# Another order of the expert pairs in a mixture-of-experts stage: pairs of 96 and of 128 rows take turns

## The chip, the cores and the metric

One core of a Trainium2 chip runs the whole program as one launch. The metric is device microseconds of that launch, the median of several runs; less is better. The profile is one more execution, recorded by the hardware.

## What is computed

The reference is two blocks of a network on 256 tokens of width 1024, in float32. The first block (attention, a recurrent mixer, plain feed-forward layers) and the mixer of the second block come first and are not touched. What matters is the last stage, a mixture of 32 experts of which each token uses 4:

```python
def moe_ffn(h, router_w, router_b, w_gu, b_gu, w_down, b_down):
    logits = hf @ router_w + router_b
    top_logit, top_idx = lax.top_k(logits, TOP_K)          # 4 of 32
    gates = jax.nn.softmax(top_logit, axis=-1)
    ...
    def expert_block(args):
        xb, e = args
        y = clamped_swiglu(xb @ w_gu[e] + b_gu[e])         # 1024 x 2048
        return y @ w_down[e] + b_down[e]                   # 1024 x 1024
    ...
    out = jax.ops.segment_sum(y_rows * row_gate, row_tok)
```

The result is added to the residual and the sum is normalised. All 32 experts are used, so 32 x 12 MB of weights are read.

## The kernel before

The expert stage is the method `moe`, some 1000 us at the end of the program. A routing step ranks the experts 2 to 31 by the number of their tokens; experts 0 and 1 are fixed as the first two, so that their weights can be loaded before the routing is known. A **pair** is two ranks that are worked on together: the list `pairs` (L2086) puts rank 0 with rank 1, 64 rows each, and then rank 1 + b with rank 32 - b for b from 1 to 15. The first of the two has 96 rows for b below 8 and 64 rows from 8 on; the second always has 32. So there are seven pairs of 128 rows (ranks 2 to 8 in front), eight of 96 rows (ranks 9 to 16 in front), and the first with 64 + 64. Rows beyond an expert's place are left to a later branch (`moe_beyond`), which is not entered with these inputs.

The loop at L2280 walks through `pairs` in the order of the list. For each rank it reads the expert's number from a small table (`moe_expert`, L2322, on SyncE) and asks for its weights: `wload` (L146) issues eight loads of 1024 KB for the up projection and four for the down projection, each into one of 16 buffers of 1 MB that go round (tag `big`). SyncE (SP) issues these loads in order; a load waits until the matmuls of the load 16 places before have read their buffer, and for earlier loads on its lane. Nothing else moves in quantity, so the loads of weights run ahead of TensorE by at most 16 buffers, which is two thirds of a pair.

For each expert `up` (L2129) multiplies the gathered rows with the gate and up weights, adding the biases by small matmuls on `bgu` (L2144), and then forms the clamped product on DVE, ACT and POOL (L2161 to L2165). `down` (L2178) turns the product with the help of the identity (`turned`, L2173, evicted as `moeaT`), multiplies it with the down weights and scales it. The activations are the stationary operand and the weights stream: an expert of 64 rows streams 512 columns per matmul on half of the array, one of 32 rows 256 columns on a quarter. An expert of 96 rows is a part of 64 and one of 32, and reads every weight tile with both; so the time of TensorE for a tile grows with the rows, and the bytes do not.

While a pair is worked on, its first expert also carries the selection for the next pair (`pair`, `gather`, L2197, matmuls at L2207 into `xg`), and its second expert the addition of the previous pair's result (`scatter`, L2119). The closing activation of a pair is that of `put` at L175 on ACT. A scheduler that knows the dependences lays out each engine's instructions, so the gather's matmuls stand between others. In the pair after the first, `moe_bias` (L2345, matmuls at L2358) adds the biases of the down projection.

Of the kernel before, what the change touches and what calls it, by code (L numbers as in the profile page):

```python
# [50 lines left out]
class Kern:  # L51
# [2025 lines left out]
    def moe(self):  # L2077
# [5 lines left out]
        dn_of = lambda e: self.wload(wdn[e], 0, 8, 0, D)  # L2083


        pairs = [((0, 64), (1, 64))] + [((1 + b, 96 if b < 8 else 64), (32 - b, 32)) for b in range(1, 16)]  # L2086
        rows = dict(chain.from_iterable(pairs))
        most = lambda r: 256 if r < 2 else min(256, 1024 // (r - 1))
        first = [gu_of(0), dn_of(0), gu_of(1)]
# [465 lines left out]
```

## Time and profile before

| | us |
|---|---|
| median of 3 runs | 3098.86 |
| fastest and slowest of them | 3097.3 and 3103.04 |
| the profiled execution, its own time | 3102.66 |
| span of its records | 3100.9 |
| the first pair closes at | 2147.37 |
| the last pair closes at | 3079.49 |

A window is a stretch of the span. Its row gives its length, the busy time of each engine with the number of its instructions, the granted clock of TensorE as a share of full speed (0.5 is 1.2 GHz, 1.00 is 2.4 GHz; a number between is a mean over both), the busy share of the DMA engines and the bytes that they moved per second. A busy TensorE is not one at its peak, since its matmuls overlap. The clock of the whole span was 0.916. The windows by pair below are those of places 1 to 10, of place 15 and of the end behind it, place 0 being the pair of experts 0 and 1.

### The profile page before, as it was taken

The page shows a single profiled execution, that of the slowest core. Times are in us where ns is not written, and L with a number is a line of the kernel's source. Part 1 is how long each engine was busy: PE and PEld are TensorE (multiplying, and loading weights), DVE is VectorE, ACT ScalarE, POOL GpSimd, SP SyncE. Part 2 cuts the span into 40 slices and gives each one's busy share as a digit, 9 for nine tenths or more (in the row PEclk, how much of TensorE's full clock was granted, in tenths as well). Part 3 has the DMA queues.
Part 4 walks back from the last instruction along what each step waited for, and adds up shares of the span by engine and source line. Part 5 has one row for each costly group of instructions (what it writes and reads, how often), then busy time and mean ns, then how long its engine had stood idle before and what let it go on. Part 6 is the DMA issues. An engine that isn't in the chain of part 4 may idle for free. (4 is left out here: it accounts for less than half of the span.)

```text
span 3100.9 us, 47594 instructions
## 1 busy us (share of the span) xinstructions
PE 2765.1 (89%) x19070; PEld 1795.3 (58%) x19070; DVE 1490.4 (48%) x3210; ACT 882.5 (28%) x1827; POOL 517.4 (17%) x774
## 2 busy tenths in 40 slices
PE   7998989999979788987899988989999999998775
PEld 4873468888847555654798966763444433443332
DVE  4426465555567655764655878651222222222121
ACT  4223334223235343433454634530100000000001
POOL 0002310111100543543100322111100000000000
PEclk9998999999988897887899998989999999879887
DMA  6226741233221233432456323369999999999997
GB/s 227 96 92 211 273 144 55 95 95 95 86 86 42 75 108 98 108 95 81 144 190 204 118 62 113 125 248 360 381 411 382 373 377 372 416 417 416 416 417 290
DMA packets 254007, 650.74 MB, mean 210 GB/s; under 512 B 68816, under 2 KB 129616, under 8 KB 215376
## 3 DMA queue, kind: packets, MB, share of 16 engines
q1 hardware_dynamic: 239552, 632.96, 55.4%
q10 hardware_dynamic: 12432, 10.45, 1.1%
q0 software_dynamic: 1792, 4.20, 0.5%
q8 instruction: 152, 2.49, 0.3%
q14 instruction: 79, 0.65, 0.1%
HBM read 639.16 MB, written 8.39 MB: 209 GB/s over the span
## 5 line engine op out<-in xcount | busy, mean ns | idle before, releaser
L2126 PE MATMUL mm<-w,xg 128*32 128x256 f32 (+1 forms) x3904 | 434.2, 457 | 38.3 <-DMA w<-in_moe_w_gu_dram 38.3
L164 DVE TENSOR_TENSOR lo<-w,hi 128x512 fp32r<-128x512 f32 (+1 forms) x330 | 295.1, 927 | 107.7 <-ACT hi L163 93.4
L2126 PEld LDWEIGHTS mm<-w,xg 128*32 128x32 f32 (+1 forms) x3904 | 155.7, 120 | 306.0 <-issue 190.2
L163 ACT ACTIVATE hi<-w 128x512 fp32r<-128x512 f32 (+1 forms) x356 | 256.3, 770 | 236.5 <-PE tp L250 101.2
L2126 PE MATMUL mm<-w,moeaT 128*32 128x256 f32 (+1 forms) x1952 | 258.7, 500 | 8.7 <-DVE moeaT L95 3.8
L2162 ACT ACTIVATE moes<-moeg 128x256 f32<-128x256 f32 (+1 forms) x39 | 19.9, 510 | 653.6 <-DVE moeg L2161 653.6
L2161 DVE TENSOR_SCALAR moeg<-mm 128x256 f32<-128x256 f32 (+1 forms) x39 | 21.1, 541 | 349.7 <-PE mm L2126 349.3
L250 PE MATMUL mm<-mlo,hi 128*128 128x512 f32 (+1 forms) x512 | 173.4, 339 | 0.7 <-DVE mlo L173 0.7
L249 PE MATMUL mm<-mhi,hi 128*128 128x512 f32 (+1 forms) x512 | 173.1, 340 | 0.0
L251 PE MATMUL mm<-mhi,lo 128*128 128x512 f32 (+1 forms) x512 | 172.2, 337 | 0.0
L2126 PEld LDWEIGHTS mm<-w,moeaT 128*32 128x32 f32 (+1 forms) x1952 | 79.8, 128 | 140.8 <-issue 108.8
L251 PE MATMUL tp<-hi,aTl 128*128 128x512 f32 x384 | 151.7, 395 | 0.0
L250 PE MATMUL tp<-lo,aTh 128*128 128x512 f32 x384 | 151.3, 394 | 0.0
L249 PE MATMUL tp<-hi,aTh 128*128 128x512 f32 x384 | 151.1, 393 | 0.0
L2164 POOL TENSOR_TENSOR moeg<-moeg,moes 128x256 f32<-128x256 f32 (+1 forms) x39 | 37.4, 959 | 580.6 <-ACT moes L2162 566.0
L2195 DVE TENSOR_TENSOR moey<-mm,moegate 32x256 f32<-32x256 f32 (+1 forms) x122 | 60.5, 496 | 138.8 <-PE mm L2126 127.3
L164 POOL TENSOR_TENSOR lo<-w,hi 128x512 fp32r<-128x512 f32 (+1 forms) x26 | 51.8, 1994 | 348.0 <-ACT hi L163 293.9
L250 PEld LDWEIGHTS mm<-mlo,hi 128*128 128x128 f32 x512 | 96.4, 188 | 12.8 <-DVE mlo L173 1.1
L249 PEld LDWEIGHTS mm<-mhi,hi 128*128 128x128 f32 x512 | 96.0, 188 | 12.3 <-issue 0.5
L251 PEld LDWEIGHTS mm<-mhi,lo 128*128 128x128 f32 x512 | 96.3, 188 | 11.4
L2139 POOL TENSOR_SCALAR moesel<-moetk,moeown 128x320 fp32r<-128x320 f32 (+1 forms) x39 | 40.8, 1046 | 317.3 <-PE mm L2144 278.0
L249 PE MATMUL cv<-hT2h,hi 128*128 128x256 f32 x288 | 84.3, 293 | 8.8 <-DVE cvy L1754 8.8
(866 smaller groups left out, 5897.8 us busy)
## 6 DMA issues: line engine op xcount, KB each, us to landing
w<-in_moe_w_gu_dram SPq DMA_DIRECT2D x256, 1024.0 KB, 15.0
w<-in_moe_w_down_dram SPq DMA_DIRECT2D x128, 1024.0 KB, 16.6
w<-in_mlp_w_dram SPq DMA_DIRECT2D x64, 1024.0 KB, 5.4
w<-in_ada_w_dram SPq DMA_DIRECT2D x48, 1024.0 KB, 5.0
w<-in_w_in_dram SPq DMA_DIRECT2D x26, 1024.0 KB, 5.2
adaw<-in_ada_w_dram SPq DMA_DIRECT2D x48, 512.0 KB, 4.1
w<-in_ab_w_in_dram SPq DMA_DIRECT2D x14, 1024.0 KB, 5.1
w<-in_rw_w_rkv_dram SPq DMA_DIRECT2D x8, 1024.0 KB, 5.1
```

Source lines behind the costliest of these rows:

```text
L163: nc.scalar.activation(h, raw, AF.Copy)
L164: (eng or nc.vector).tensor_sub(l, raw, hi)
L249: nc.tensor.matmul(out, l[0], r[0], start=start, stop=False)
L250: nc.tensor.matmul(out, l[0], r[1], start=False, stop=False)
L251: nc.tensor.matmul(out, l[1], r[0], start=False, stop=stop)
L2126: return 8 * n, lambda p, c, l, r, s, st: nc.tensor.matmul(p[c * n:(c + 1) * n, :8 * n], l, r, start=s, stop=st, tile_position=(0, c * n))
L2139: nc.gpsimd.tensor_scalar(sel.bitcast(FR), takes[n], own[:, r:r + 1], None, op0=OP.mult)
L2161: nc.vector.tensor_scalar(g, pg[:, :w], 7.0, None, op0=OP.min)
L2162: nc.scalar.activation(s, g, AF.Sigmoid, scale=1.702)
L2164: nc.gpsimd.tensor_mul(g, g, s)
L2195: nc.vector.tensor_mul(y[:, cs], py[c * n:(c + 1) * n, :w], gate[c * n:(c + 1) * n, cs])
```

## The change

The list of pairs is written in another order. No pair is changed, and neither are the rows of a rank or the number of any instruction. After the first pair come the pairs with b = 8, 1, 9, 2, 10, 3, 11, 4, 12, 5, 13, 6, 14, 7, 15: of 96 rows, of 128, of 96, and so on, with one of 96 rows at the end. It was b = 15 at the end before, too.

```diff
-        pairs = [((0, 64), (1, 64))] + [((1 + b, 96 if b < 8 else 64), (32 - b, 32)) for b in range(1, 16)]
+
+        pairs = [((0, 64), (1, 64))] + [((1 + b, 96 if b < 8 else 64), (32 - b, 32))
+                                        for b in (8, 1, 9, 2, 10, 3, 11, 4, 12, 5, 13, 6, 14, 7, 15)]
```

Lines below it move by two. On SP the rows of the program stay as they were. On TensorE whole pairs change places. Just behind the first pair, TensorE before works on an expert of 96 rows; `w,xg` are products with the up weights (64x512 for a part of 64 rows, 32x256 for one of 32), `moebd,moeGT` the biases:

```order
L2126 MATMUL mm<-w,xg 64x512 x7
L2126 MATMUL mm<-w,xg 32x256 x13
L2358 MATMUL tp<-moebd,moeGT 128x512 x4
L2126 MATMUL mm<-w,xg 32x256 x3
L2126 MATMUL mm<-w,xg 64x512 x8
L2126 MATMUL mm<-w,xg 32x256 x16
```

The same place of the changed program, with the gather for the next pair (`moeoh,xnm`) behind it:

```order
L2128 MATMUL mm<-w,xg 64x512 x15
L2360 MATMUL tp<-moebd,moeGT 128x512 x4
L2128 MATMUL mm<-w,xg 64x512 x17
L2209 MATMUL tp<-moeoh,xnmh 128x128 x2
L2209 MATMUL tp<-moeoh,xnml 128x128 x2
```

The expert with 96 rows, eight tiles read by 32 + 64 matmuls in all, has made room for one of 64 rows with 32 matmuls (the trace shows two records for each of them); the biases' products stay in the first products of this pair.

The second place is on TensorE where the pair after a pair of 128 rows begins. Before it is another one of 128 rows (`moeaT` are the last down products of the pair that ends, 32 rows):

```order
L2126 MATMUL mm<-w,moeaT_18716 32x256 x8
L2207 MATMUL tp<-moeoh,xnml 128x128
L2207 MATMUL tp<-moeoh,xnmh 128x128 x2
L2207 MATMUL tp<-moeoh,xnml 128x128 x2
L2207 MATMUL tp<-moeoh,xnmh 128x128 x2
L2207 MATMUL tp<-moeoh,xnml 128x128
L2144 MATMUL mm<-bguh,moesel 128x256
L2144 MATMUL mm<-bgul,moesel 128x256
L2144 MATMUL mm<-bguh,moesel 128x256
L2144 MATMUL mm<-bgul,moesel 128x256
L2207 MATMUL tp<-moeoh,xnml 128x128
L2126 MATMUL mm<-w,xg 64x512 x4
```

In the changed program a pair of 96 rows begins there, its first expert in one piece, with the turning of its product and the scatter behind it:

```order
L2128 MATMUL mm<-w,moeaT_18590 32x256 x8
L2209 MATMUL tp<-moeoh,xnmh 128x128
L2209 MATMUL tp<-moeoh,xnml 128x128 x2
L2209 MATMUL tp<-moeoh,xnmh 128x128 x2
L2209 MATMUL tp<-moeoh,xnml 128x128 x2
L2128 MATMUL mm<-w,xg 64x512 x32
L2175 MATMUL tp<-ident,moeu_18721 128x128 x4
L2121 MATMUL tp<-moeyh,moegt 128x512
```

The second half of the biases for a part of 32 rows is gone there, and the eight up tiles of the pair follow in one run of matmuls.

## Rows read from the trace of the kernel before

**Rows 1.** The page, the span in 40 equal slices: rate of the transfers.
```profile
GB/s 227 96 92 211 273 144 55 95 95 95 86 86 42 75 108 98 108 95 81 144 190 204 118 62 113 125 248 360 381 411 382 373 377 372 416 417 416 416 417 290
```

**Rows 2.** Windows by pair: length; PE, PEld, DVE, ACT, POOL busy; clock; DMA share; GB/s.
```profile
2147.40:2214.30 66.90, 63.88 (x562) 29.27 (x562) 19.29 (x40) 4.58 (x9) 11.53 (x11) 0.95 0.84 330
2214.30:2279.30 65.00, 61.42 (x583) 30.72 (x581) 16.62 (x37) 6.12 (x13) 7.08 (x7) 0.97 1.02 416
2279.30:2343.10 63.80, 58.29 (x552) 25.83 (x552) 16.87 (x36) 4.82 (x9) 5.80 (x6) 1.00 1.01 408
2343.10:2411.30 68.20, 62.81 (x552) 27.58 (x552) 16.28 (x35) 5.31 (x10) 5.80 (x6) 0.92 0.94 379
2411.30:2479.70 68.40, 62.83 (x552) 27.49 (x552) 16.87 (x36) 4.84 (x10) 5.80 (x6) 0.93 0.92 367
2479.70:2548.60 68.90, 62.84 (x553) 27.68 (x553) 16.15 (x36) 5.26 (x11) 5.79 (x6) 0.93 0.93 372
2548.60:2617.50 68.90, 64.09 (x558) 27.34 (x560) 17.49 (x38) 5.46 (x11) 5.63 (x6) 0.93 0.92 366
2617.50:2665.80 48.30, 43.35 (x352) 20.82 (x350) 13.25 (x28) 4.54 (x9) 3.99 (x4) 0.96 1.02 418
2665.80:2724.20 58.40, 52.90 (x348) 26.18 (x346) 13.33 (x28) 4.49 (x8) 3.99 (x4) 0.77 1.02 416
2724.20:2786.00 61.80, 54.05 (x354) 25.62 (x352) 13.25 (x28) 4.55 (x9) 3.99 (x4) 0.78 1.02 417
...
3019.00:3079.50 60.50, 44.69 (x308) 15.92 (x304) 10.69 (x18) 2.80 (x5) 1.98 (x2) 0.86 0.92 374
3079.50:3100.90 21.40, 3.78 (x8) 2.48 (x8) 7.06 (x12) 6.40 (x9) 0.00 (x0) 0.50 0.21 78
```

**Rows 3.** Timeline of ACT: the closing activation of place 0 and of place 15.
```profile
2147.37 1.15 ACT L175 ACTIVATE moeyh<-moey,moetg 128x1024 fp32r<-128x1024 f32 x1 [10.03 <-DVE moey L2195]
...
3079.49 1.15 ACT L175 ACTIVATE moeyh<-moey,moetg 96x1024 fp32r<-96x1024 f32 x1 [10.92 <-DVE moey L2195]
```

**Rows 4.** The page, DMA issues: count, KB of each, us to landing.
```profile
w<-in_moe_w_gu_dram SPq DMA_DIRECT2D x256, 1024.0 KB, 15.0
w<-in_moe_w_down_dram SPq DMA_DIRECT2D x128, 1024.0 KB, 16.6
```

**Rows 5.** Waits of SP's queue (total, times, longest), first 2300 to 2620, then 2700 to 3060.
```profile
SPq L155 <- PE mm L2126: 240.8, 111, 9.9
...
SPq L155 <- DMA w<-in_moe_w_gu_dram: 106.4, 66, 2.4
SPq L155 <- DMA w<-in_moe_w_down_dram: 94.3, 48, 2.1
SPq L155 <- PE mm L2126: 45.9, 31, 5.0
```

**Rows 6.** Timeline of TensorE at place 9: start, length, instruction, idle time before it.
```profile
2701.68 1.07 PE L2126 MATMUL mm<-w,xg 128*32 128x256 f32 x16 [0.79 <-DMA w<-in_moe_w_gu_dram]
```

**Rows 7.** Groups by shape, 2150 to 3101 us: busy, mean ns of one, idle before.
```profile
L97 ACT ACTIVATE moeaT<-tp 128x512 f32<-128x512 f32 x11 | 6.5, 593 | 24.1 <-PE tp L2173 24.1
```

**Rows 8.** Windows of the two experts of place 5, then of place 8.
```profile
2411.30:2455.10 43.80, 41.16 (x307) 13.74 (x307) 7.78 (x14) 3.50 (x6) 2.91 (x3) 0.92 0.88 353
2455.10:2479.70 24.60, 21.67 (x248) 13.75 (x246) 9.09 (x23) 1.35 (x4) 2.89 (x3) 0.93 0.99 392
2617.50:2644.80 27.30, 24.48 (x112) 9.20 (x111) 6.02 (x8) 2.38 (x3) 2.34 (x2) 0.94 1.02 417
2644.80:2665.80 21.00, 18.86 (x246) 11.62 (x246) 7.23 (x20) 2.17 (x6) 1.65 (x2) 1.00 1.02 418
```

**Rows 9.** Timelines: SP and the biases at place 1, TensorE at place 8.
```profile
2142.50 31.17 SPq L155 DMA_DIRECT2D w<-in_moe_w_gu_dram  x8
...
2155.73 4.94 PE L2358 MATMUL tp<-moebd,moeGT 32*128 32x512 f32 x8 [1.15 <-DMA moebd<-in_moe_b_down_dram]
...
2615.34 13.95 PE L2126 MATMUL mm<-w,xg 128*64 128x512 f32 x64
```

## The prediction, made before the changed kernel ran

> Two names first. A **large pair** has 96 + 32 = 128 rows, a **small pair** 64 + 32 = 96. Place 0 is the pair of experts 0 and 1, places 1 to 15 follow. Before, places 1 to 7 are large and 8 to 15 small; the change makes them small, large, small, ..., small.
>
> **What bounds the kernel now.** I read the slices of the whole span first, then one window per pair, then the two halves of a pair, then the waits of SP's queue. In the slices the expert stage is the last third, and there the rate of the loads is not level: it reaches 416 to 417 GB/s in the last slices, yet 360 to 411 earlier [rows 1]. The windows by pair say where [rows 2]; their edges are the starts of the activation that closes a pair (L175), the first at 2147.37 and the last at 3079.49 us [rows 3]. From place 8 on the loads run at 416 to 418 GB/s whatever the tensor engine does: this is the level that they reach and hold. Each pair needs two experts of 8 + 4 loads of 1024 KB [rows 4], that is 24 loads or 25.2 MB, and 25.2 MB at 417 GB/s is **60.4 us**. Places 9, 10 and 15 take 58.4, 61.8 and 60.5 us: a small pair is paced by its loads. A large pair is not: places 4 to 7 take 68.2 to 68.9 us while the loads fall to 366 to 379 GB/s. So the stage has two bounds that take turns, TensorE in the large pairs and the loads in the small ones, and what one side has to spare in its half of the stage is not there in the other.
>
> The queue's waits confirm the sides. Between 2300 and 2620 us SP waits 240.8 us for matmuls that free one of the 16 buffers; between 2700 and 3060 us it waits 106.4 + 94.3 us for earlier loads to land and only 45.9 us for matmuls [rows 5]. In the small pairs it is TensorE that waits, a little at each tile [rows 6].
>
> The idle time of the loads in each pair is its length times the share missing to 417 GB/s: 14.0 us at place 1 (66.9 x 87/417), 0.2 at 2, 1.4 at 3, 6.2, 8.2, 7.4 and 8.4 at 4 to 7, nothing from place 8 on. Together **45.8 us**.
>
> **What the change does to it.** It adds and removes no work: each pair keeps its two experts, its rows and its 24 loads; matmuls, loads and transposes are as many as before. On SP the order of instructions is the same row for row; only the numbers of the experts that it reads differ. On TensorE whole pairs move, and with them the gather for the next pair, which is spread in the second expert's last products: a small pair now gathers 128 rows for the large one behind it, a large pair 96. Four evictions of turned activations go from ACT to DVE and four back. DVE, ACT and POOL are busy under a third of each pair [rows 2], so I cost these swaps at nothing; one takes 0.593 us on ACT [rows 7], so eight laid wholly open would be 4.7 us, or as much gained.
>
> *Large pairs.* Could a large pair still stall its loads? Count tiles (one load each), 2.52 us per tile at 417 GB/s. At place 5 the 96-row expert takes 43.8 us, in which 17.4 tiles could land, and uses 12: the stock grows by 5.4. The 32-row expert takes 24.6 us, 9.8 tiles against 12: minus 2.2 [rows 8]. So a large pair ends 3.2 up, and a row of them fills the 16 buffers; the loads then stall in every first half, as the 353 GB/s there show. A small pair at place 8, with its data there, takes 27.3 + 21.0 us, 19.2 tiles against 24: minus 4.8. Behind each large pair now comes a small one, so two together lose 1.6 tiles, and the stock falls instead of filling. It was at most 16 less the 5.4 it still grew, about 10, when a large pair began. A small pair takes it to about 5, the next large pair peaks near 11 and ends near 9, the next small one takes it to 4, and so on down. The peak never reaches 16, so the stalls of places 3 to 7 go: 1.4 + 6.2 + 8.2 + 7.4 + 8.4 = 31.6 us. I take all of it.
>
> *The first pair.* Place 1 is another matter: SP needs 31.17 us for the eight loads issued from 2142.50 us, because the buffers were already full when it began, while TensorE ran the 96-row expert with the 4.94 us of the biases' products between [rows 9]. With a small pair here the eight tiles are freed by 64 matmuls in 13.95 us [rows 9] plus the same 4.94, about 19 us for eight tiles, 2.4 us per tile and so the pace of the loads. The idle time there lies between nothing (buffers freed at the loads' pace) and the whole 14.0. I take 3, near the lower end, because the freeing pace is measured on the same instructions.
>
> *What is late next.* With the loads never idle, TensorE must keep up. Large pairs at the mean of places 4 to 7, 68.6 us, and small ones at place 8's 48.3 us give 7 x 68.6 + 8 x 48.3 + 4.9 for the biases = 871.5 us for places 1 to 15. The loads give 932.1 (3079.5 - 2147.4) - 45.8 + 3 = 889.3 us. So the loads decide, with 18 us to spare. Two pairs together are 116.9 us of TensorE against 120.8 of loads: after the stock is used up, the small pairs wait some us each and the large ones none. The last pair is the same small pair as before, and the 21.4 us behind it stay.
>
> *Clock.* Places 9 and 10 were granted 0.77 and 0.78, a mixture of 1.2 and 2.4 GHz, when TensorE waited at tiles; place 8 with its data there 0.96 and place 3 1.00 [rows 2]. Waits will now be spread over all small pairs, so large pairs may begin at 1.2 GHz. That is held by the 18 us, and it corrects itself: a slower large pair lets more tiles land, and the next small pair waits less.
> The Trainium skill, "TensorE: Matmul & The Clock Gate", section "HAM oscillation — how this bites in real kernels", speaks against the change here: waiting for data between groups of matmuls throttles the array again at each tile. By that rule alone the small pairs would go like places 9 and 10 and large ones slower, which is the slower rival below.
> The Trainium skill, "DMA: Bandwidth & Descriptors", section "Specifications", puts a core's share of HBM at about 358 GB/s. By it a pair's loads would take 70.3 us, more than a large pair does, and the change would bring nothing (the rival of no effect); the trace does not agree, since places 8 to 10 hold 416 to 418 GB/s.
>
> **Sum.** 31.6 + 0.2 at place 2 + 11.0 of place 1 = **42.8 us** less. The profiled execution took 3102.66 us with a span of 3100.9; 42.8 less is a span of 3058 and 3060 us. It lies 3.8 above the median of the three runs, 3098.86, from which I take the forecast: **3056 us**.
>
> **The rivals.**
> *TensorE becomes the bound* (chance 0.13). If a small pair needs more than (889.3 - 4.9 - 480.2)/8 = 50.5 us with its data there, TensorE decides. Halfway between place 8 and place 9, 53.3 us, gives 22 us more: 3078. For it: only one small pair in the trace ran with its data there, so 48.3 rests on one sample. Against it: it had a granted clock of 0.96 and held a gather and a scatter like any other.
> *The loads still stall in large pairs* (0.08), if the stock at their start is nearer 16 than I count. Half the mean of places 4 to 7, 3.8 us, in each of seven is 26 us: 3082. For it: place 3, with full rate before it, already lost 1.4. Against it: place 2 lost 0.2 only.
> *No effect* (0.04): the loads run below 380 GB/s in places 4 to 7 because TensorE is busy and not because buffers are full. Then each large pair keeps its time wherever it stands and each small one its 60: 3093 to 3105. Against it: at place 2 they held 416 GB/s beside 61.4 us of matmuls in 65.0 [rows 2].
> *Slower* (0.05): the clock. If waits at tiles keep TensorE at the mixture of place 9 and a small pair itself needs 58.4 us, then 7 x 68.6 + 8 x 58.4 + 4.9 = 952.3, 20 us over the 932.1 of now: 3119. It decides from 55.9 us per small pair on. Against it: place 9's 58.4 us are the time of its loads at 416 GB/s, not of its matmuls.
>
> **How the numbers follow.** The forecast has 0.70. Its own ends are 45.8 us less (3053) and 31.8 less (3067, all of place 1 lost again), widened by the 3 us by which runs differ. The range takes in part of the first rival: 3049 to 3074. About 0.2% is what a measurement of this kernel can tell from no change: faster 0.91 (forecast and first two rivals), same 0.04, slower 0.05.
>
> **What would show it.** Right: a rate of 415 GB/s or more in every window from the end of place 0 to the last load; large pairs of 63 to 69 us, small ones of 50 to 58; SP waiting for loads, not for matmuls, in the middle of the stage; the same 21 us at the end. Wrong: windows of large pairs under 400 GB/s (second rival), loads at full rate but a last pair long after the last load, or small pairs over 56 us while SP waits for matmuls (first rival and the slower one).

## The result, and the profile after

The changed kernel takes **3065.67 us** (median of four runs, 3057.41 to 3071.95) beside 3100.95 us of the kernel before on the same chip. The ratio is 0.988, 95% interval 0.9855 to 0.9900: 1.2% faster. The forecast was 3056 us with a range of 3049 to 3074.

The page of the profile after, the rate of the transfers in 40 equal slices of the span (it answers to [rows 1]):

```profile
GB/s 229 98 92 211 273 151 55 97 97 96 83 78 54 68 116 94 103 84 108 105 200 177 140 103 103 64 261 315 397 417 416 416 416 416 417 416 417 416 417 275
```

From the thirtieth slice on there is one level up to the end of the stage; the dip to 372 to 382 that stood in the middle is gone. The windows by pair, as [rows 2] (length; PE, PEld, DVE, ACT, POOL busy; clock; DMA share; GB/s), places 1 to 5, the last two and the end:

```profile
2152.00:2209.40 57.40, 53.48 (x394) 26.57 (x390) 16.79 (x35) 5.17 (x11) 9.81 (x9) 0.94 0.98 392
2209.40:2272.90 63.50, 58.68 (x554) 25.65 (x556) 16.85 (x36) 4.66 (x9) 5.65 (x6) 1.00 1.02 416
2272.90:2323.80 50.90, 44.56 (x352) 22.50 (x348) 13.26 (x28) 4.46 (x8) 4.16 (x4) 0.93 1.02 417
2323.80:2391.60 67.80, 63.12 (x554) 27.27 (x556) 16.28 (x35) 5.15 (x10) 5.65 (x6) 0.92 1.02 416
2391.60:2441.00 49.40, 43.12 (x352) 20.89 (x348) 13.60 (x28) 4.25 (x8) 4.16 (x4) 0.97 1.02 416
...
2927.70:2992.50 64.80, 59.95 (x524) 23.09 (x524) 15.65 (x32) 3.75 (x7) 4.73 (x5) 0.92 1.02 416
2992.50:3044.80 52.30, 40.37 (x302) 16.30 (x302) 10.87 (x18) 2.81 (x5) 1.98 (x2) 0.90 0.85 346
3044.80:3065.90 21.10, 3.47 (x8) 2.14 (x8) 7.06 (x12) 6.39 (x9) 0.00 (x0) 0.54 0.21 79
```

Large pairs still take 63.5 to 68.0 us, small ones now 49.4 to 57.4, and the loads do not care which of the two runs: 416 or 417 GB/s in each window from place 2 to place 14. Only place 1 is below, at 392. (The last pair's 346, like the 374 of place 15 before, is no stall: all its loads are issued by 3022.3 us, and the rate falls as the last ones land.)

The stage runs from the closing activation of place 0 to that of place 15. ACT's timeline after, as [rows 3]:

```profile
2151.99 1.15 ACT L175 ACTIVATE moeyh<-moey,moetg 128x1024 fp32r<-128x1024 f32 x1 [10.19 <-DVE moey L2197]
...
3044.78 1.15 ACT L175 ACTIVATE moeyh<-moey,moetg 96x1024 fp32r<-96x1024 f32 x1 [11.30 <-DVE moey L2197]
```

Places 1 to 15 take **892.8 us** where they took 932.1 (39.3 less; forecast 889.3), and the end behind them 21.1 (before 21.4). I call this difference of the two closings "the stage" below. It is a sharper measure than the whole time: place 0 closes 4.6 us later than in the profile of before, although of the work up to there only the rows that place 0 gathers for the next pair have changed (96 instead of 128).

SP's queue after, total wait, times and longest, between 2300 and 2620 us, where [rows 5] had 240.8 us for matmuls:

```profile
SPq L155 <- DMA w<-in_moe_w_gu_dram: 85.8, 51, 3.3
SPq L155 <- DMA w<-in_moe_w_down_dram: 71.6, 37, 3.4
SPq L155 <- PE mm L2128: 64.9, 44, 6.1
```

The queue now waits 157 us for earlier loads to land and 65 for buffers. It has become, in the middle of the stage, what it was before only among the small pairs.

### The profile page after: what moved, and what is told of

Its sections match the earlier page's. It is cut to its first block, busy times and chain, and to the rows that moved or that the text cites. A ratio compares the mean times of both kernels' runs of the same rounds, so it can differ in the third digit from the quotient of the medians.

```text
span 3065.9 us, 47588 instructions
## 1 busy us (share of the span) xinstructions
PE 2751.7 (90%) x19070; PEld 1796.0 (59%) x19070; DVE 1493.2 (49%) x3210; ACT 881.7 (29%) x1827; POOL 517.1 (17%) x774
## 5 line engine op out<-in xcount | busy, mean ns | idle before, releaser
L2128 PE MATMUL mm<-w,xg 128*32 128x256 f32 (+1 forms) x3904 | 420.4, 447 | 10.1 <-DMA w<-in_moe_w_gu_dram 10.1
L2128 PE MATMUL mm<-w,moeaT 128*32 128x256 f32 (+1 forms) x1952 | 252.3, 478 | 12.0 <-ACT moeaT L97 4.4
L2163 DVE TENSOR_SCALAR moeg<-mm 128x256 f32<-128x256 f32 (+1 forms) x39 | 21.1, 541 | 321.7 <-PE mm L2128 321.4
```

Source lines behind the costliest of these rows:

```text
L2128: return 8 * n, lambda p, c, l, r, s, st: nc.tensor.matmul(p[c * n:(c + 1) * n, :8 * n], l, r, start=s, stop=st, tile_position=(0, c * n))
L2163: nc.vector.tensor_scalar(g, pg[:, :w], 7.0, None, op0=OP.min)
```

## The experiments

In the orders below, the numbers are the b of the places 1 to 15; 1 to 7 are large pairs, 8 to 15 small ones. The first lines of the diffs are those of the changed kernel.

**The same kernel again.** No edit; it shows how far the result itself repeats.

> The changed kernel once more, beside other orders on one chip. Theory (the loads of weights are idle while large pairs fill the 16 buffers, and taking turns ends that): 3060 to 3070 us, loads at 416 to 417 GB/s from the second place on. Rival (a large part of the difference comes from other stages or other executions): a time over 3080.

Measured: 3064.37 us (3054.68 to 3068.02), ratio 0.9867 [0.9844, 0.9890]; the stage 893.2 us beside 892.8. So single executions differ by some 13 us in the whole, while the stage of the two profiled ones repeats within half a microsecond. The loads ran at 415 GB/s or more from place 3 to 14, but at 411 at place 2, 1 us of idle time that the first profile does not have.

**Two and two.**

```diff
-(8, 1, 9, 2, 10, 3, 11, 4, 12, 5, 13, 6, 14, 7, 15)
+(8, 9, 1, 2, 10, 11, 3, 4, 12, 13, 5, 6, 14, 7, 15)
```

> Two small pairs, then two large ones, and so on: 8, 9, 1, 2, 10, 11, 3, 4, 12, 13, 5, 6, 14, 7, 15. Theory (a stock of tiles in 16 buffers): two large pairs raise the stock from 0 to 3.2 and 6.4 with a peak of 8.6, so the loads never stall; the time is that of strict turns within 5 us, 3060 to 3071. Rival (each change from one kind of pair to the other is what helps): half of the changes, so about half of the gain, 3080 to 3086.

Measured: 3063.36 us, ratio 0.9880 [0.9859, 0.9901]; the stage 892.8 us, with loads at 413 to 417 GB/s from place 2 on. The rival, by which each change from one kind of pair to the other brings its share, would have given half the gain (3080 to 3086) and falls. The strict turn is not needed; what counts is that not too many of one kind stand in a row.

**Fours.**

```diff
-(8, 1, 9, 2, 10, 3, 11, 4, 12, 5, 13, 6, 14, 7, 15)
+(8, 9, 10, 11, 1, 2, 3, 4, 12, 13, 14, 5, 6, 7, 15)
```

> Four small, four large, three small, three large, one small. Theory: the fourth large pair in a row peaks near 15 tiles and loses 2 to 6 us; the last small pair begins with about 9.6 tiles in stock, so TensorE ends it some 12 us behind the last load: 14 to 18 us more than strict turns, 3077 to 3088. Rival (any mixing is as good as any other): 3060 to 3071.

Measured: 3080.03 us, ratio 0.9927 [0.9897, 0.9957]; the stage 910.4 us, 17.6 more than with turns, as expected. Windows of the third and fourth large pair in a row, and of the last pair:

```profile
2500.40:2569.50 69.10, 62.82 (x554) 27.55 (x554) 16.77 (x37) 4.81 (x10) 5.81 (x6) 0.93 1.00 405
2569.50:2638.20 68.70, 64.10 (x558) 27.41 (x560) 16.85 (x37) 6.05 (x12) 5.65 (x6) 0.93 0.93 373
...
3002.60:3051.80 49.20, 39.48 (x303) 16.56 (x302) 10.69 (x18) 2.82 (x5) 1.99 (x2) 0.90 0.75 305
```

The pairs before these two, the first and second of the row, ran at 416. The stall sets in with the third large pair (2.0 us of idle time) and is whole with the fourth (7.2, more than the 2 to 6 expected); in the second row, of three, the third ran at 383 GB/s. This is what a stock of loaded tiles does that grows until it meets the 16 buffers. The last pair is short, 49.2 us, because the second row of large pairs left its data behind; that does not give back what was lost.

**Small pairs all first.**

```diff
-(8, 1, 9, 2, 10, 3, 11, 4, 12, 5, 13, 6, 14, 7, 15)
+(8, 9, 10, 11, 12, 13, 14, 1, 2, 3, 4, 5, 6, 7, 15)
```

> Seven small pairs, then the seven large ones, then the last small one. Theory: the loads pace the small pairs from the second or third on (60 us each), then the row of large pairs fills the buffers and stalls the loads from its fourth, and the last small pair begins with a full stock and is paced by TensorE: places 1 to 15 take about 57 + 50 + 5 x 60.4 + 7 x 68.3 + 48.3 = 935 us, that is no gain, 3096 to 3108. Rival (a small pair behind the first one is enough): 3060 to 3090.

Measured: 3095.85 us, ratio 0.998 [0.9958, 1.0001]; the stage 919.1 us. So small pairs at the start bring at most a third of the gain in the stage (13.0 of 39.3 us) and nothing that the whole times tell from no change, and the rival that saw the gain there (3060 to 3090) falls. The time is just under the lower end I wrote down, and the stage was 16 us shorter than I had worked out. The large pairs, fourth to sixth of seven, and the last pair:

```profile
2743.70:2811.90 68.20, 62.79 (x552) 27.54 (x552) 16.28 (x35) 5.32 (x11) 5.81 (x6) 0.92 1.00 403
2811.90:2880.30 68.40, 62.84 (x553) 27.49 (x553) 16.87 (x36) 4.88 (x10) 5.82 (x6) 0.93 0.94 376
2880.30:2949.20 68.90, 62.83 (x554) 27.65 (x554) 16.17 (x36) 5.25 (x11) 5.82 (x6) 0.93 0.93 372
...
3013.80:3061.20 47.40, 37.80 (x302) 15.89 (x302) 10.68 (x18) 2.78 (x4) 1.99 (x2) 0.93 0.78 316
```

Coming with an empty stock, the first three large pairs run at 416 GB/s and the stall starts with the fourth. The first three also take 65.4, 65.0 and 63.8 us and the seventh 64.6, where I had counted 68.3 for each: the seven take 464.3 us instead of 478.1, which is 14 of the 16 us. The last pair took 47.4, much as the 48.3 that I had counted.

**One small pair at place 1, the rest as before.** It was meant to take the first pair's 11 us by itself.

```diff
-(8, 1, 9, 2, 10, 3, 11, 4, 12, 5, 13, 6, 14, 7, 15)
+(8, 1, 2, 3, 4, 5, 6, 7, 9, 10, 11, 12, 13, 14, 15)
```

> Only the first step of the change: one small pair moved to place 1, then the seven large ones, then the seven small ones left. Theory: 3.4 us lost at place 1 instead of 14, and the seven large pairs in a row fill the buffers again and lose 0, 0, 1, 6, 8, 8, 8 us: about 10 us gained, 3087 to 3095. Rival (the gain comes from the small pair right behind the first one, which begins the stage with a lead): 3060 to 3075.

Measured: 3103.36 us (twelve runs), ratio 0.9999 [0.9979, 1.0019]; the stage 931.0 us beside 932.1. **The expectation missed:** no gain. Place 1 itself does what I said (56.6 us at 393 GB/s, 3.3 us idle instead of 14.0). What became of the 11 us stands in the windows of places 3, 4 and 8:

```profile
2269.10:2337.10 68.00, 62.70 (x552) 27.24 (x552) 16.28 (x35) 5.37 (x10) 5.81 (x6) 0.92 0.98 390
2337.10:2402.50 65.40, 59.84 (x552) 26.52 (x552) 16.87 (x36) 4.84 (x10) 5.81 (x6) 0.97 0.97 389
...
2607.60:2682.70 75.10, 70.40 (x554) 31.12 (x556) 17.46 (x38) 5.49 (x12) 5.65 (x6) 0.83 0.93 368
```

The loads stall from place 3 on, the second large pair, and go on so through place 8. Idle time by pair: 3.3, 0.2, 4.4, 4.4, 7.8, 7.2, 7.8, 8.8, 1.2, together 45.1 us, against 45.8 before. The sum is the same to a microsecond. (The 75.1 us of place 8 are not the reason for it: its low clock, 0.69, is in its second half, 31.0 us long, where the loads ran at 400 GB/s and lost little over 1 us.) A microsecond of load time won at one pair only fills the stock earlier, and a row of seven large pairs gives it back. The gain at place 1 is a gain only if small pairs further on make room for it.

**A large pair at place 1, then turns.** The other half of the same question.

```diff
-(8, 1, 9, 2, 10, 3, 11, 4, 12, 5, 13, 6, 14, 7, 15)
+(1, 8, 2, 9, 3, 10, 4, 11, 5, 12, 6, 13, 7, 14, 15)
```

> Turns, but with a large pair at place 1: 1, 8, 2, 9, 3, 10, 4, 11, 5, 12, 6, 13, 7, 14, 15. Theory: the loads lose 14 us at place 1 as before, and nothing behind it: 10 to 11 us more than strict turns with a small pair in front, 3073 to 3080. Rival (place 1 is not a term of its own): 3060 to 3070.

Measured: 3077.47 us, ratio 0.9919 [0.9900, 0.9937]; the stage 903.5 us, 10.7 more than the changed kernel's, as expected. Places 1 and 2:

```profile
2147.90:2214.60 66.70, 63.80 (x561) 28.61 (x562) 19.14 (x40) 4.49 (x9) 11.59 (x11) 0.95 0.84 328
2214.60:2267.00 52.40, 47.67 (x384) 24.97 (x380) 13.81 (x30) 5.38 (x10) 4.46 (x5) 0.97 1.02 417
```

Place 1 is idle for 66.7 x 89/417 = 14.2 us, as it was before, and every window from place 2 to 14 holds 416 or 417. So of the 39.3 us about 11 come from place 1 and 28 from the row of large pairs being broken up; and the first needs the second, as the run above shows.

**Less work for TensorE, the same loads.** In the changed order, rows 64 to 95 of seven experts are left out, so all pairs from place 1 on have 96 rows. (The other lines of the edit, which set the limits of the ranks so that `moe_beyond` stays out, are not shown.)

```diff
-        pairs = [((0, 64), (1, 64))] + [((1 + b, 96 if b < 8 else 64), (32 - b, 32))
+        pairs = [((0, 64), (1, 64))] + [((1 + b, 64), (32 - b, 32))
```

> The changed order with 64 rows instead of 96 in the seven large pairs; rows 64 to 95 of seven experts are left out. All the loads stay, TensorE has some 7 x 20 = 140 us less to do. Theory (behind place 0 the loads decide everything): at most the 3.4 us that the loads still lose at place 1 can be had, 3058 to 3067, and every pair takes about 60 us. Rival (TensorE still decides part of the stage): 3045 or less.

Measured: 3054.9 us, ratio 0.985 [0.9815, 0.9882]; the stage 889.9 us, 2.9 less than with all rows. (The time as a whole is 3 us below my expectation; in this execution place 0 closed at 2142.1, 10 us earlier than in the profile after.) The loads ran at 416 or 417 GB/s from place 2 to 14. Seven large pairs of 63.5 to 68 us were turned into small ones and the stage moved by 3 us: TensorE does not decide it.

**TensorE's waits covered, in both orders.** While a product is turned, TensorE waits 1.8 to 1.9 us for VectorE with nothing else in reach. A pin on the order of three kinds of matmul puts the gather and the scatter, work that is there anyway, between the up products and the turning. All loads and all rows stay. The edit at the first transpose; those at the first matmul of the gather and of the scatter are alike and not shown:

```diff
-                    nc.tensor.transpose(tp[:, j * 128:(j + 1) * 128], u[:, j * 128:(j + 1) * 128], self.ident)
+                    t = nc.tensor.transpose(tp[:, j * 128:(j + 1) * 128], u[:, j * 128:(j + 1) * 128], self.ident)
+                if j == 0:
+                    tc.keep_in_program_order(t)
```

In the old order:

> The old order of pairs with all loads, but TensorE's instructions pinned: the gather for the next pair stands between an expert's up products and the turning of its result, and the scatter likewise in the second expert, as in the kernel with fewer loads. Theory (large pairs outlast their loads by the waits at the turning and the lower clock behind them, not by their matmuls): large pairs fall from 68 to about 60 us, paced by the loads; only the 14 us at place 1 stay; places 1 to 15 in 896 to 906 us against 932, whole time 3065 to 3080. Rival (the matmuls of 128 rows outlast the loads by themselves): large pairs stay at 64 us or more, whole time 3090 to 3105.

In the new order:

> The changed order with the same pins. Theory (behind place 0 the loads decide, so a faster TensorE is worth next to nothing here): places 1 to 15 in 884 to 893 us, whole time 3053 to 3066. Rival (in turns TensorE is still late somewhere): 880 us or less, 3050 or less.

Measured, old order: 3079.16 us, ratio 0.9929 [0.9905, 0.9953], the stage 905.0 us. The rival that large pairs would stay at 64 us and more falls: of the six behind place 1 one takes 64.5 us, the others 58.5 to 62.8. The pins do what they were made for; TensorE's waits at the turning, 57.0 us over the whole stage before, are now (total, times, longest):

```profile
PE tp L2175 <- DVE moeu L2167: 2.8, 2, 2.2
```

Places 1, 2, 5 and the first small pair of the old order with the pins:

```profile
2162.40:2229.40 67.00, 63.69 (x562) 29.32 (x562) 19.21 (x40) 4.62 (x10) 11.64 (x11) 0.95 0.84 328
2229.40:2287.90 58.50, 55.48 (x552) 26.72 (x550) 15.89 (x35) 5.18 (x11) 7.03 (x7) 1.00 1.02 416
...
2413.90:2476.70 62.80, 58.21 (x552) 26.03 (x552) 16.55 (x36) 4.58 (x9) 5.83 (x6) 0.97 1.01 410
...
2598.50:2642.40 43.90, 40.28 (x346) 19.53 (x344) 12.80 (x28) 4.29 (x9) 4.02 (x4) 1.00 1.02 415
```

Large pairs of 58.5 to 64.5 us at 406 to 416 GB/s: the row of large pairs is hardly a TensorE stretch any more, and 27 of the 39 us are had without changing the order. What remains is mostly place 1, at 328 GB/s as ever.

Measured, new order: 3060.96 us, ratio 0.9878 [0.9853, 0.9903], the stage 891.8 us, 1.0 less than without the pins. Two neighbouring pairs, a large and a small one:

```profile
2543.90:2605.00 61.10, 58.86 (x556) 25.91 (x556) 15.83 (x35) 5.05 (x10) 5.68 (x6) 0.97 1.02 417
2605.00:2664.90 59.90, 45.34 (x348) 19.84 (x346) 13.08 (x28) 4.31 (x8) 4.18 (x4) 0.94 1.02 416
```

Here the same pins are worth nothing that can be measured: the large pairs become shorter, 61 to 64 us, the small ones from place 5 on longer, 58 to 61.5, at an unchanged 416 GB/s from place 4 on. An improvement of TensorE that brought 27 us under TensorE's bound brings 1 us under that of the loads. The two changes are two ways to the same gain, not two gains.

**Fewer loads, in both orders.** To see what TensorE needs when the loads decide nothing, the down weights are not loaded from place 1 on; the down products read up tiles instead (eight loads of an expert's twelve remain).

```diff
-                    gu, dn = (first[2 * i] if b == 0 else gu_of(e)), (first[1] if b == i == 0 else dn_of(e))
+                    gu = first[2 * i] if b == 0 else gu_of(e)
+                    dn = (first[1] if b == i == 0 else dn_of(e)) if b == 0 else (lambda f, gu=gu: gu(f // 2)[:, f % 2 * D:f % 2 * D + D])
```

In the new order:

> The changed order, but from place 1 on the down weights are not loaded: the down products read the first four up tiles of the same expert instead. 16 loads per pair, 40 us at 417 GB/s, so TensorE decides in both orders. Theory: places 1 to 15 take the sum of TensorE's times, 871.5 us, against 889 to 893 with all loads; whole time 3035 to 3050, and the same as in the old order within 4 us. Rival (the new order has waits or clock losses of its own on TensorE): 6 us or more slower than the old order without these loads.

In the old one:

> The old order with the same loads left out (down products read the first four up tiles of the same expert). Theory: without a shortage of loads the order does not matter: 3035 to 3050, within 4 us of the changed order without these loads. Rival (large pairs first is worse for TensorE itself): 10 us or more slower than the changed order without these loads.

Measured: 2922.23 us in the new order, ratio 0.942, the stage 754.1; 2940.23 us in the old one, ratio 0.9475, the stage 771.3. **Both expectations missed by over 90 us.** I had taken the 68.6 and 48.3 us of a pair for the time of its matmuls. With fewer loads a large pair takes 57 to 60 us and a small one 42; place 4 and a small pair of the old order:

```profile
2327.40:2384.20 56.80, 55.71 (x553) 26.89 (x552) 15.90 (x35) 5.20 (x10) 6.54 (x7) 1.00 0.74 291
...
2598.70:2640.60 41.90, 40.82 (x352) 20.29 (x350) 12.81 (x28) 4.21 (x8) 3.96 (x5) 1.00 0.99 395
```

The reason is not the loads alone. With them gone, the program was scheduled differently: in the large pairs the gather and the scatter stand between the up products and the turning, and the waits there are nearly gone. TensorE's waits at the turning in the old order with all loads, 2343 to 2617 us, four large pairs (total, times, longest):

```profile
PE tp L2173 <- DVE moeu L2165: 14.8, 8, 1.9
```

With fewer loads, 2212 to 2499 us, five large pairs:

```profile
PE tp L2173 <- DVE moeu L2165: 2.3, 5, 0.5
```

That these waits, and not the number of loads, make the difference is what the pinned kernels above were built to show, and they do: with all loads, a large pair at 58.5 us (place 2 of the old order). The 17 us between the two orders here lie in the small pairs (360 us for eight in the old order, 344.5 in the new one), where the last five of the old order took 44 to 48 us with waits at the turning (18.6 us between 2682 and 2918). So the two kernels differ in their layout, and the pair of them is no test of the order by itself.

## Why the prediction was right, point by point

**The two bounds that take turns: right.** The stage went from 932.1 to 892.8 us with the same matmuls and loads, by bringing the loads from 45.8 us of idle time to 3.4. Less TensorE work (all pairs small, 2.9 us) and a faster TensorE (1.0 us) change nothing further.

**The stalls of places 3 to 7: right.** I took all 31.6 us, and in the profile after none is left in any pair from place 2 on. The first half of a large pair ran at 353 GB/s before [rows 8]. The two halves of place 4 after:

```profile
2323.80:2367.50 43.70, 41.12 (x306) 13.61 (x306) 7.65 (x14) 3.43 (x6) 2.92 (x3) 0.92 1.02 415
2367.50:2391.60 24.10, 22.01 (x250) 13.66 (x250) 8.63 (x22) 1.72 (x4) 2.74 (x3) 0.93 1.02 418
```

The halves are as long as before, 43.7 and 24.1 us against 43.8 and 24.6; it is the buffers that are free now.

**Place 1: right in size, partly by luck.** Idle there 57.4 x 25/417 = 3.4 us, where I had taken 3 between the ends 0 and 14. SP's eight loads, which took 31.17 us [rows 9], after, and the products that free their buffers:

```profile
2147.12 23.29 SPq L155 DMA_DIRECT2D w<-in_moe_w_gu_dram  x8
...
2151.57 7.08 PE L2128 MATMUL mm<-w,xg 128*64 128x512 f32 x30
2160.31 5.18 PE L2360 MATMUL tp<-moebd,moeGT 32*128 32x512 f32 x8 [1.67 <-DMA moebd<-in_moe_b_down_dram]
2165.42 9.78 PE L2128 MATMUL mm<-w,xg 128*64 128x512 f32 x34
```

I had counted 19 us for the eight tiles, the pace of the loads; they took 23.6, because the products ran slower than at place 8 (16.9 us instead of 13.95) and waited 1.67 us for the biases. Nor could my sign of being right, 415 GB/s in every window from the end of place 0 on, hold there by my own 3 us of idle time: the window has 392.

But I told this gain as one that stands by itself, and it does not: alone it is worth nothing (3103.36 us).

**The ledger of the stock: right in direction, its ceiling wrong.** I counted -4.8 tiles for a small pair and a ceiling of 16. At place 1 a small pair takes 56.6 us with the biases in it; at 393 GB/s that is 21.2 tiles landed for 24 used, -2.8 (these two numbers from the run with one small pair ahead). In that run the loads stalled already in the second large pair. By my numbers the stock there is about 10 at the end of place 0, less 2.8, plus 3.2, plus the 5.4 of a first half, which just reaches 16; yet 4.4 us were lost. (My own steps have a slip too: 10 less 4.8 plus 3.2 is 8.4, not "near 9".)

A load holds its buffer from issue to landing, 15.0 us [rows 4] or six loads' time, so buffers in flight are not stock, and the ceiling for landed tiles must lie below 16. The trace of before shows it, if issues, landings and used tiles are counted (to about one tile, since a quarter of the landings have no record and are put between their neighbours). At the ends of places 4 to 7 some 9 tiles lie landed and unread and 6 loads are in flight, 15 of 16 buffers together. In the first half of place 5 the loads in flight then fall from 6 to 2. The rate falls behind the first wait at the turning; three windows with about 4, 2 and 2 loads in flight:

```profile
2430.00:2435.00 5.00, 5.00 (x46) 1.46 (x42) 1.38 (x2) 0.63 (x1) 0.23 (x1) 1.00 1.00 414
...
2440.00:2445.00 5.00, 5.00 (x17) 1.37 (x20) 0.00 (x0) 0.38 (x1) 0.00 (x0) 0.53 0.28 112
2445.00:2450.00 5.00, 5.00 (x44) 1.51 (x36) 0.00 (x0) 0.00 (x0) 0.00 (x0) 1.00 0.66 220
```

By this count the loads falter here at some 12 to 14 landed tiles and not at 16, and they do so where TensorE waits and then runs at a granted clock of 0.53. In the changed order, counted the same way, 8 tiles lie landed at the end of place 0, and then 5, 7 and 2 at the ends of places 1 to 3, where I had 10, and then 5, 9 and 4. Each large pair begins with 5 (place 2) or 1 to 3 (later), and so stays below the ceiling, though with the loads in flight 15 buffers are taken again at the ends of places 1, 2 and 4. More or fewer buffers, which would move the ceiling, were not tried.

**"18 us to spare" on TensorE: the verdict right, its ground wrong.** The 871.5 us were not the time of the matmuls. About 11 of each large pair's 68.6 us are not needed, by the 57 to 58 us of the large pairs with fewer loads. Place 3 before, with the same waits at the turning but a granted clock of 1.00, took 63.8 us; so by this estimate some 5 of the 11 us are the lower clock and 6 the waits and the layout around them. In the profile after the waits are still there, 1.82 and 1.89 us at place 4, since nothing waits for TensorE long enough to matter. Over the whole stage they are 59.6 us after and 57.0 before; what fell is the wait for the up weights. Before:

```profile
PE tp L2173 <- DVE moeu L2165: 57.0, 28, 2.8
...
PE mm L2126 <- DMA w<-in_moe_w_gu_dram: 38.3, 41, 2.0
```

After:

```profile
PE tp L2175 <- DVE moeu L2167: 59.6, 29, 2.8
...
PE mm L2128 <- DMA w<-in_moe_w_gu_dram: 10.1, 9, 1.4
```

**The clock: the rival fell.** Small pairs after were granted 0.90 to 0.97, not the 0.77 and 0.78 of places 9 and 10 [rows 2], so waiting was less harmful than the slower rival needed. Where every pair waits for its loads, in the kernel with less TensorE work, single pairs do fall to 0.76 to 0.78, and even those cost nothing while the loads hold their level. The lower clock of a TensorE that waits for data, which the Trainium skill describes ("TensorE: Matmul & The Clock Gate", "HAM oscillation — how this bites in real kernels"), is seen in these runs (0.77 at place 9 before) but decides no time here.

**The rival of no effect fell as well.** Loads hold 416 or 417 GB/s beside large pairs with 58 to 63 us of matmuls in them, so it was full buffers and not a busy TensorE that held them down. The 358 GB/s that the Trainium skill ("DMA: Bandwidth & Descriptors", "Specifications") gives as a core's share of HBM is passed in each of these windows by a program that runs on one core.

**The size.** The time came out 9.7 us above the forecast, within its range. In the stage, 3.5 us: the loads hold 416 more often than the 417 I divided by (a quarter of a percent of some 890 us, about 2 us), place 1 adds 0.4, about 1 is unassigned. The rest is ahead of the stage and in the scatter of executions: place 0 closed 4.6 us later in the profile after than in that of before, and the same program took 3054.68 to 3071.95 us in eight runs. By medians the gain is 35 to 39 us, of which I had expected 42.8.

## What to carry to other kernels

Where two bounds take turns within a stage, compare the whole sums of each side with the stage's time, and then ask how long a row of one kind the buffers can bridge: here two large pairs in a row cost next to nothing behind small ones, a third or a fourth began to stall, and behind place 0, where 8 tiles lie ready, it was sooner. Idle time won at one place is a gain only if the stock has room behind it; otherwise the next full buffer gives it back. And a stage's length per piece is not the work in it: look for short waits before taking it as a bound; to cover them may be the same gain by another way.

## What the runs showed of the hardware that I had not expected

- **The same short waits went with two clocks.** In the kernel before, places 3 and 5 have the same waits at the turning. Place 3 was granted 1.00 and took 63.8 us; place 5 was granted 0.93, with 0.53 in the 5 us shown above, and took 68.4. The down products behind the first wait, at place 3 and at place 5:

```profile
2304.88 0.63 PE L2173 MATMUL tp<-ident,moeu 128*128 128x128 f32 x4 [1.82 <-DVE moeu L2165]
2306.29 1.07 PE L2126 MATMUL mm<-w,moeaT 128*64 128x512 f32 x2 [0.78 <-DVE moeaT L95]
...
2307.66 11.54 PE L2126 MATMUL mm<-w,moeaT 128*64 128x512 f32 x94
...
2436.91 0.63 PE L2173 MATMUL tp<-ident,moeu 128*128 128x128 f32 x4 [1.82 <-DVE moeu L2165]
2438.32 1.97 PE L2126 MATMUL mm<-w,moeaT 128*64 128x512 f32 x2 [0.78 <-DVE moeaT L95]
...
2440.84 13.38 PE L2126 MATMUL mm<-w,moeaT 128*64 128x512 f32 x94
```

  So at place 5 the same 96 records take 2.7 us more, at a lower clock. With the waits covered, at place 2 of the old order with the pins, a window granted 1.00:

```profile
2257.93 11.54 PE L2128 MATMUL mm<-w,moeaT 128*64 128x512 f32 x96 [1.02 <-ACT moeaT L97]
```

  Large pairs with the waits covered and a clock of 1.00 take 57 to 60 us. Why the clock fell behind these waits at place 5 and not at place 3, no run shows.

- **The same instructions ahead of the stage take up to 24 us more or less.** Place 0 closed at 2138.0 us in the pinned kernel of the new order and at 2162.4 in that of the old one, at 2141.4 to 2152.0 in all others. All of these 24 us are there already 172 us earlier, at the first `cath` activation of L175 (1966.4 and 1990.5 us), far ahead of what the pins touch. The same kernel's stage, between two closings, repeated within 0.4 us.
- **The loads' level is very steady:** 416 or 417 GB/s in all pairs of nearly 800 us after (411 in one pair of the repeat), whether TensorE was granted 0.91 or 1.00.
